# Mixture of experts on one core: the next expert's rows turned and split behind the fifth chunk of this expert's first products

## The chip, the cores and the metric

The kernel runs on one core of one Trainium2 chip. The metric is the time of one launch on the device, in microseconds (us). The engines of the core run side by side, each through its own list of instructions, and wait for one another by semaphores: TensorE (PE) for matrix products, VectorE (DVE) and ScalarE (ACT) for element-wise work, GpSimd (POOL), and SyncE (SP), which here only issues transfers (DMA).

## The reference

The program is two transformer blocks on 512 tokens of width 1024. The first has two layers of mixed attention and a gated MLP. The second has a recurrent part, banded and memory attention, and ends in a routed mixture of 32 experts. Only the experts matter here. Each token goes to two experts; expert e computes, for the rows `xb` routed to it,

```
g = xb @ w_gate[e]                      # 1024 -> 512
u = xb @ w_up[e]                        # 1024 -> 512
y = (silu(g) * u) @ w_down[e]           # 512 -> 1024
```

`y` is weighted by the router and added to the token's row; a last norm follows. All is in float32.

## The kernel before

A product of float32 numbers is made of three products of rounded parts: each operand is split into a high part, its value rounded, and a low part, the rest; high by high, high by low and low by high are summed. So each weight and each row goes through a copy on ACT (high part) and a subtraction on DVE (low part) first.

The experts are run one after another with up to 96 rows each (`CAP`). The weights of one expert come in 12 chunks of 512 KB: eight of gate and up together (`e_gu`, 128 of the 1024 input features each) and four of down (`e_dn`). SP loads each into one of 28 raw buffers (`ewr`), ACT casts the high part `ewh` (L1478), DVE subtracts the low part `ewl` (L1480). Of `ewh` and of `ewl` there are three buffers each (`NH`), so a chunk's cast can only start when the products of the chunk three places before it are done.

One expert's run (`Experts.run`) has these steps:

- Turning: the gathered rows `gx` (96 x 1024) are transposed on PE, eight pieces into two PSUM banks `s` (L1500), and split into `xh` on ACT (L186) and `xl` on DVE (L187). Then the gather for the expert two places on is issued on POOL (`then()`).
- First products: for each of the eight chunks six matmuls, into `pg` (gate, L1512) and `pu` (up, L1513).
- `z`: ACT takes the silu of `pg` (L1515), DVE multiplies it by `pu` (L1516).
- Second products: `z` is transposed on PE into `pt` (L1520, four pieces) and split into `zh` on ACT and `zl` on DVE (L186, L187). Then 24 matmuls with the four down chunks (L1530).
- ACT scales the result into `y` (L1539, two halves), POOL adds it to the output in memory (L1540).

`run` is a generator. Its `yield`s cut it into pieces, and the loop in `moe_block` calls the pieces of two experts in turn, so that the first two chunks of expert e+1 stand ahead of the down products of expert e. The five PSUM banks for products are given out in turn, so `pu` of expert e+1 gets the bank of `pg` of expert e, and must wait until the silu has read it.

The order of the calls is not yet the order on the engines. The framework schedules the recorded instructions by its own estimate of when each can run, fixes one list for each engine, and adds the waits. The lists shown below are those.

Of the kernel before, what the change touches and what calls it, by code (L numbers as in the profile page):

```python
# [1281 lines left out]
NE = 32  # L1282
CAP = 96
LAST = 2
# [161 lines left out]
class Experts:  # L1446
# [41 lines left out]
    def run(self, i, gu, dn, sidx, w, r, y=None, then=lambda: None):  # L1488


        B, nc, wk = self.B, self.B.nc, self.wk
        mm = nc.tensor.matmul
        flat = lambda t: t.rearrange("p k n -> p (k n)")
        xh = wk.tile([P, KD, CAP], F32R, tag="xh", name="xh", bufs=self.nw)
        xl = wk.tile([P, KD, CAP], F32R, tag="xl", name="xl", bufs=self.nw)
        for a in range(2):
            pt = B.bank("t", "s")[:, :4 * CAP]
            for j in range(4):
                k = 4 * a + j
                nc.tensor.transpose(pt[:, j * CAP:(j + 1) * CAP], self.gx[i][:, k * P:(k + 1) * P],  # L1500
                                    B.ident[:CAP, :CAP])
            s = slice(4 * a, 4 * a + 4)
            B.split(pt, flat(xh[:, s]), flat(xl[:, s]))
        then()
        pg, pu = B.acc()[:CAP], B.acc()[:CAP]
        for k in range(KD):
            if k == 2:
                yield
            wh, wlo = gu(k)
            for x, ww, last in ((xh, wh, False), (xh, wlo, False), (xl, wh, k == KD - 1)):  # L1510
                first = k == 0 and ww is wh and x is xh
                mm(pg, x[:, k], ww[:, :T], start=first, stop=last)  # L1512
                mm(pu, x[:, k], ww[:, T:], start=first, stop=last)  # L1513
        z = wk.tile([CAP, T], F32, tag="z", name="z", bufs=self.nw)
        self.silu = nc.scalar.activation(z, pg, AF.Silu, scale=r)  # L1515
        nc.vector.scalar_tensor_tensor(z, pu, r, z, op0=ALU.mult, op1=ALU.mult)  # L1516
        yield
        pt = B.pst()[:, :4 * CAP]
        for j in range(4):
            nc.tensor.transpose(pt[:, j * CAP:(j + 1) * CAP], z[:, j * P:(j + 1) * P], B.ident[:CAP, :CAP])  # L1520
        zh = wk.tile([P, 4, CAP], F32R, tag="zh", name="zh", bufs=self.nw)
        zl = wk.tile([P, 4, CAP], F32R, tag="zl", name="zl", bufs=self.nw)
        self.zl = B.split(pt, flat(zh), flat(zl))
        pd = [B.acc()[:CAP], B.acc()[:CAP]]
        for k in range(4):
            wh, wlo = dn(k)
            for x, ww, last in ((zh, wh, False), (zh, wlo, False), (zl, wh, k == 3)):
                first = k == 0 and ww is wh and x is zh
                for a in range(2):
                    mm(pd[a], x[:, k], ww[:, a * T:(a + 1) * T], start=first, stop=last)  # L1530
        if y is not None:
            y.append([wk.tile([CAP, D], F32R, tag="y" + g, name="y" + g, bufs=LAST) for g in "hl"])
            for a in range(2):
                B.gsplit(pd[a], w, [t[:, a * T:(a + 1) * T] for t in y[-1]])
            yield
            return
        y = wk.tile([CAP, D], F32, tag="y", name="y", bufs=self.nw)
        for a in range(2):
            nc.scalar.mul(y[:, a * T:(a + 1) * T], pd[a], w)  # L1539
        nc.gpsimd.indirect_dma_start(out=self.y2[:, :], out_offset=bass.IndirectOffsetOnAxis(ap=sidx, axis=0),  # L1540
                                     in_=y, in_offset=None, bounds_check=T - 1, oob_is_err=False,
                                     compute_op=ALU.add)
        yield
# [73 lines left out]
def moe_block(B, dense, out):  # L1617

    tc, nc, I = B.tc, B.nc, B.I
    with ExitStack() as cx:  # L1620
# [66 lines left out]
        def run(e, y=None):  # L1687
            then = (lambda: ex.gather(e % NG, idx[:, e + NG:e + NG + 1])) if e + NG < NE else lambda: None
            return ex.run(e % NG, lambda k: ex.load(gu[e * D + k * P:e * D + (k + 1) * P, :]),
                   lambda k: ex.load(dn[e * T + k * P:e * T + (k + 1) * P, :]), idx[:, e:e + 1], wl[:, 0, e:e + 1],  # L1690
                          wl[:, 1, e:e + 1], y, then)
# [9 lines left out]

        pick, ys = [], []
        prev, now = None, run(0)
        next(now)
        for e in range(NE):
            next(now)
            ex.hold = None, None
            if e + 1 < NE:
                then = run(e + 1, ys if e + 1 >= NE - LAST else None)
                next(then)  # L1710
            if e < NE - 2:
                next(now)
            elif e == NE - 1:
                next(prev)
                next(now)
            prev, now = now, then
# [30 lines left out]
def build(tc, I, out):  # L1747
    with ExitStack() as ctx:
        dr = ctx.enter_context(tc.tile_pool(name="drm", bufs=1, space=bass.MemoryType.DRAM))
        B = Block(tc, I, ctx)  # L1750
        B.kd = dr.tile([KD, P, 256], F32, name="kd")
        B.vd = dr.tile([2, P, D], F32, name="vd")
        first = first_block(B)
        moe_block(B, lambda h3: second_block_dense(B, first, h3), out)
# [158 lines left out]
```

## Time and profile before

| what | value |
|---|---|
| three timed runs | 2436.26, 2440.36, 2441.43 us; median 2440.36 us |
| profiled execution, its own time | 2438.89 us |
| its span, first to last instruction | 2437.1 us |
| PE busy over the span | 2284.5 us (94%) |
| DVE busy | 1768.8 us (73%) |
| ACT busy | 1402.7 us (58%) |
| chain that ended last | PE 71%, DVE 11%, issue 8%, ACT 6%, DMA 3% |

The launch's own time is 1.8 us longer than the span. The chain of work that ended last is followed back from the last instruction, at each step to what released it. The experts take the last quarter of the span, from about 1824 to about 2420 us. In the rows below a time is counted from the start of the span; "idle before" is how long the engine had nothing running just before the row, and the arrow names what ended that.

### The profile page before, as it was taken

The numbers are of one execution on the slowest core, as the hardware profiler recorded it, in microseconds if no ns is written. First come the engines' busy times: TensorE is split into PE (matmuls) and PEld (weight loads), VectorE is DVE, ScalarE is ACT, GpSimd is POOL, SyncE is SP. The second block draws the span as 40 slices with busy tenths as digits, with TensorE's granted clock in tenths as the row PEclk, the third lists the DMA queues.
The fourth block names the chain that finished last, engine by engine and source line by source line (L and its number), as shares of the span: only waits on it lengthen the run. The fifth ranks groups of instructions, "written<-read, shape, count | busy, mean of one in ns | idle before, by whom it ended". The sixth has DMA issues, their size and how long they took to land.

```text
span 2437.1 us, 33968 instructions
## 1 busy us (share of the span) xinstructions
PE 2284.5 (94%) x12341; PEld 1877.2 (77%) x12341; DVE 1768.8 (73%) x3246; ACT 1402.7 (58%) x2279; POOL 142.9 (6%) x136
## 2 busy tenths in 40 slices
PE   6888989999999899899999998999979999999998
PEld 6878968888888789788888887978756666666665
DVE  7899878745756897664434467687658888888888
ACT  4576764322333867643223446655427888888886
POOL 0000000000000000000000000100011111111110
PEclk9999999999999999999999999999979999999999
DMA  9623415635643111032233232214379999999992
GB/s 325 190 87 105 140 60 170 202 115 180 195 143 93 44 62 55 33 104 95 80 111 95 80 98 79 61 57 151 110 270 325 362 364 358 357 354 353 353 348 93
DMA packets 131872, 417.83 MB, mean 171 GB/s; under 512 B 22937, under 2 KB 30105, under 8 KB 131696
## 3 DMA queue, kind: packets, MB, share of 16 engines
q1 hardware_dynamic: 122832, 401.03, 48.2%
q0 software_dynamic: 8864, 14.54, 2.2%
q8 instruction: 99, 1.62, 0.3%
q14 instruction: 77, 0.63, 0.1%
HBM read 411.46 MB, written 20.19 MB: 177 GB/s over the span
## 4 chain that ended last, share of the span: by engine, by line
PE 71%; DVE 11%; issue 8%; ACT 6%; DMA 3%; SPq 0%; POOL 0%; DVEq 0%; ACTq 0%; POOLq 0%
PE acc L191 12%; PE acc L192 12%; PE acc L193 12%; PE acc L1512 8%; PE acc L1530 7%; PE acc L1513 7%; PE acc L490 2%; PE acc L491 2%; PE acc L492 2%; DVE wl L177 2%; PE s L396 1%; PE pv L457 1%; PE pt L444 1%; DVE wm L384 1%; ACT wh L176 1%
## 5 line engine op out<-in xcount | busy, mean ns | idle before, releaser
L176 ACT CAST wh<-wr 128x1024 fp32r<-128x1024 f32 (+2 forms) x284 | 272.9, 963 | 454.1 <-PE acc L192 356.0
L1480 DVE TENSOR_TENSOR ewl<-ewr,ewh 128x1024 fp32r<-128x1024 f32 x384 | 463.7, 1221 | 72.7 <-ACT ewh L1478 51.2
L177 DVE TENSOR_TENSOR wl<-wr,wh 128x1024 fp32r<-128x1024 f32 (+2 forms) x284 | 317.2, 1118 | 229.2 <-ACT wh L176 222.7
L1478 ACT CAST ewh<-ewr 128x1024 fp32r<-128x1024 f32 x384 | 397.6, 1052 | 88.5 <-PE acc L1513 54.3
L191 PE MATMUL acc<-hh,wh 128*128 128x512 f32 (+1 forms) x1088 | 411.0, 380 | 5.2 <-ACT hh L186 4.1
L192 PE MATMUL acc<-hl,wh 128*128 128x512 f32 (+1 forms) x1088 | 414.4, 381 | 0.0
L193 PE MATMUL acc<-hh,wl 128*128 128x512 f32 (+1 forms) x1088 | 411.5, 379 | 1.9 <-DVE wl L177 1.9
L191 PEld LDWEIGHTS acc<-hh,wh 128*128 128x128 f32 x1088 | 204.6, 189 | 48.3 <-ACT hh L186 4.7
L193 PEld LDWEIGHTS acc<-hh,wl 128*128 128x128 f32 x1088 | 206.1, 189 | 42.6 <-DVE wl L177 2.7
L192 PEld LDWEIGHTS acc<-hl,wh 128*128 128x128 f32 x1088 | 205.8, 189 | 40.2 <-DVE hl L187 0.2
L490 PE MATMUL acc<-wh,hh 128*128 128x256 f32 (+1 forms) x768 | 228.9, 298 | 0.0
L491 PE MATMUL acc<-wl,hh 128*128 128x256 f32 (+1 forms) x768 | 221.4, 288 | 0.0
L492 PE MATMUL acc<-wh,hl 128*128 128x256 f32 (+1 forms) x768 | 221.0, 288 | 0.0
L491 PEld LDWEIGHTS acc<-wl,hh 128*128 128x128 f32 x768 | 151.0, 197 | 2.8
L490 PEld LDWEIGHTS acc<-wh,hh 128*128 128x128 f32 x768 | 151.5, 197 | 2.0
L492 PEld LDWEIGHTS acc<-wh,hl 128*128 128x128 f32 x768 | 150.6, 196 | 0.0
L401 ACT ACTIVATE e<-e,st 128x128 f32<-128x128 f32 (+2 forms) x192 | 107.6, 561 | 69.7 <-DVE st L399 67.8
L384 DVE SCALAR_TENSOR_TENSOR wm<-wm,scb 128x1024 f32<-128x1024 f32 x96 | 116.8, 1221 | 37.3 <-DMA wm<-in_w_mod_dram 36.7
L192 PE MATMUL acc<-zl,wh 128*128 128x512 f32 (+1 forms) x363 | 141.3, 389 | 0.0
L191 PE MATMUL acc<-zh,wh 128*128 128x512 f32 (+1 forms) x363 | 141.0, 389 | 0.0
L193 PE MATMUL acc<-zh,wl 128*128 128x512 f32 (+1 forms) x363 | 140.2, 386 | 0.0
L1512 PE MATMUL acc<-ewh,xh 128*96 128x512 f32 x256 | 103.9, 406 | 12.6 <-ACT xh L186 12.6
(418 smaller groups left out, 4575.6 us busy)
## 6 DMA issues: line engine op xcount, KB each, us to landing
ewr<-in_e_gu_dram SPq DMA_DIRECT2D x256, 512.0 KB, 7.2
ewr<-in_e_dn_dram SPq DMA_DIRECT2D x128, 512.0 KB, 8.5
wm<-in_w_mod_dram SPq DMA_DIRECT2D x96, 512.0 KB, 4.2
wr<-in_w_up_dram SPq DMA_DIRECT2D x88, 512.0 KB, 3.5
wr<-in_w_qkv_dram SPq DMA_DIRECT2D x56, 512.0 KB, 3.5
wr<-in_w_down_dram SPq DMA_DIRECT2D x32, 512.0 KB, 3.6
wr<-in_w_out_dram SPq DMA_DIRECT2D x16, 512.0 KB, 3.5
wr<-in_w_down_dram SPq DMA_DIRECT2D x32, 192.0 KB, 2.3
```

The lines of the kernel that those rows point to most:

```text
L176: nc.scalar.copy(hi, raw)
L177: nc.vector.tensor_sub(lo, raw, hi)
L191: mm(ps, wh, ah, start=first, stop=False)
L192: mm(ps, wh, al, start=False, stop=False)
L193: mm(ps, wl, ah, start=False, stop=last)
L490: mm(ps, ah[:, s], wh[:, w], start=k == 0, stop=False)
L491: mm(ps, ah[:, s], wl[:, w], start=False, stop=False)
L492: mm(ps, al[:, s], wh[:, w], start=False, stop=k == KD - 1)
L1478: nc.scalar.copy(hi, raw)
L1480: nc.vector.tensor_sub(lo, raw, hi)
L1512: mm(pg, x[:, k], ww[:, :T], start=first, stop=last)
L1513: mm(pu, x[:, k], ww[:, T:], start=first, stop=last)
```

## The change

The `yield`s are set anew and the loop is changed with them. The turning of expert e+1 becomes a piece of its own, called after the fifth chunk of expert e's first products; its first two chunks are still called after the eighth. For expert 0 the turning and the first two chunks are called one after the other.

```diff
         then()
+        yield
         pg, pu = B.acc()[:CAP], B.acc()[:CAP]
         for k in range(KD):
-            if k == 2:
+            if k in (2, 5):
                 yield
...
         prev, now = None, run(0)
         next(now)
+        next(now)
         for e in range(NE):
+            next(now)
+            if e + 1 < NE:
+                then = run(e + 1, ys if e + 1 >= NE - LAST else None)
+                next(then)
             next(now)
             ex.hold = None, None
             if e + 1 < NE:
-                then = run(e + 1, ys if e + 1 >= NE - LAST else None)
                 next(then)
             if e < NE - 2:
                 next(now)
```

Below is what the engines' lists make of it, for an expert in the middle. Lines of the changed kernel are one higher there: L1513 and L1514 are the products of L1512 and L1513, L1521 is L1520, L1531 is L1530.

PE before, from the last matmuls of one expert's eighth chunk: `s` is the next expert's turning, then come its first chunk and, inside that, the transposes `pt` of this expert's z.

```order
L1513 MATMUL acc<-ewh,xl 96x512
L1500 MATMUL s<-c_ident,gx_17363 128x96 x6
L1512 MATMUL acc<-ewh,xh 96x512
L1513 MATMUL acc<-ewh,xh 96x512
L1512 MATMUL acc<-ewl,xh 96x512
L1513 MATMUL acc<-ewl,xh 96x512
L1520 MATMUL pt<-c_ident,z 128x96 x4
L1512 MATMUL acc<-ewh,xl 96x512
L1513 MATMUL acc<-ewh,xl 96x512
```

Eight more matmuls, and the down products, follow there: two of the eight transposes of `s` stand earlier, in the fifth chunk. PE in the changed kernel, from the second half of the next expert's first chunk (its three matmuls into `pg` stand ahead of the three into `pu`) to the first down products (L1531):

```order
L1514 MATMUL acc<-ewh,xh 96x512
L1514 MATMUL acc<-ewl,xh 96x512
L1514 MATMUL acc<-ewh,xl 96x512
L1513 MATMUL acc<-ewh,xh 96x512
L1514 MATMUL acc<-ewh,xh 96x512
L1513 MATMUL acc<-ewl,xh 96x512
L1514 MATMUL acc<-ewl,xh 96x512
L1513 MATMUL acc<-ewh,xl 96x512
L1514 MATMUL acc<-ewh,xl 96x512
L1521 MATMUL pt<-c_ident,z 128x96 x4
L1500 MATMUL s<-c_ident,gx_17363 128x96 x8
L1531 MATMUL acc<-ewh,zh 96x512 x2
```

The turning no longer stands ahead of its own expert's products: the list has it between the transposes of z and the down products, and it is that of the expert two places on. The transposes of z went from the middle of the next expert's first chunk to behind its second.

ACT before, from one silu (L1515) to the next: twelve casts of weight chunks (L1478), with the splits `xh` and `zh` (L186) and `y` between them.

```order
L1515 ACTIVATE z<-acc,lw 96x512
L186 CAST xh<-s 128x384 x2
L1478 CAST ewh<-ewr 128x1024
L186 CAST zh<-pt 128x384
L1478 CAST ewh<-ewr 128x1024 x5
L1539 ACTIVATE y<-acc,lw 96x512 x2
L1478 CAST ewh<-ewr 128x1024 x6
```

ACT in the changed kernel, from silu (L1516) to the next; the three casts behind it are those of the first three down chunks.

```order
L1516 ACTIVATE z<-acc,lw 96x512
L1478 CAST ewh<-ewr 128x1024 x3
L186 CAST zh<-pt 128x384
L186 CAST xh<-s 128x384 x2
L1478 CAST ewh<-ewr 128x1024 x3
L1540 ACTIVATE y<-acc,lw 96x512 x2
L1478 CAST ewh<-ewr 128x1024 x6
```

The split `zh` stood behind one cast of a down chunk and stands behind three now; DVE's list has the same shape, with `zl` behind one subtraction of a down chunk before and behind three now.

## Rows read from the trace of the kernel before

**Rows 1.** Busy time by stretch of 20 us, with granted clock, DMA share, GB/s

```profile
core 0: us, PE busy (x) PEld busy (x) DVE busy (x) ACT busy (x) POOL busy (x), PEclk, DMA share, GB/s
1820.00:1840.00 20.00, 16.92 (x63) 11.47 (x64) 12.88 (x19) 10.18 (x13) 2.60 (x2) 0.69 0.87 303
...
1960.00:1980.00 20.00, 19.59 (x92) 13.76 (x91) 17.78 (x18) 16.82 (x21) 2.49 (x2) 1.00 1.02 373
...
2380.00:2400.00 20.00, 19.59 (x92) 13.74 (x91) 17.81 (x18) 16.57 (x20) 1.43 (x1) 1.00 0.35 114
```

**Rows 2.** Tile ewr, 2370 to 2390 us: the last weight loads and their landing

```profile
L1485 SPq DMA_DIRECT2D ewr<-in_e_dn_dram x4: 328/328/328, 2369.9 to 2373.4; - x4
...
DMA to landing us min/median/max: 5.6/5.7/5.9
```

**Rows 3.** ACT in order of time: the last two casts of weights

```profile
2413.96 2.00 ACT L1478 CAST ewh<-ewr 128x1024 fp32r<-128x1024 f32 x2
```

**Rows 4.** Waits of PE, 1860 to 2395 us: total, times, longest

```profile
PE acc L1512 <- ACT xh L186: 12.3, 30, 0.4
```

**Rows 5.** PE in order of time, one expert: start, length, instruction, idle before

```profile
2061.41 0.40 PE L1513 MATMUL acc<-ewh,xl 128*96 128x512 f32 x1
2061.64 0.66 PE L1500 MATMUL s<-c_ident,gx 96*128 96x96 f32 x6
2062.71 0.47 PE L1512 MATMUL acc<-ewh,xh 128*96 128x512 f32 x1 [0.41 <-ACT xh L186]
...
2063.71 0.49 PE L1520 MATMUL pt<-c_ident,z 96*128 96x96 f32 x4
2063.99 0.46 PE L1512 MATMUL acc<-ewh,xl 128*96 128x512 f32 x1
...
2065.67 0.40 PE L1513 MATMUL acc<-ewh,xl 128*96 128x512 f32 x1
2065.90 0.62 PE L1530 MATMUL acc<-ewh,zh 128*96 128x512 f32 x2
...
2070.98 0.62 PE L1530 MATMUL acc<-ewh,zl 128*96 128x512 f32 x2
...
2074.92 0.47 PE L1512 MATMUL acc<-ewl,xh 128*96 128x512 f32 x1
...
2079.85 0.39 PE L1513 MATMUL acc<-ewh,xl 128*96 128x512 f32 x1
```

**Rows 6.** ACT in order of time, the same expert

```profile
2061.61 0.69 ACT L1515 ACTIVATE z<-acc,lw 96x512 f32<-96x512 f32 x1
2062.19 0.84 ACT L186 CAST xh<-s 128x384 fp32r<-128x384 f32 x2
...
2064.24 0.48 ACT L186 CAST zh<-pt 128x384 fp32r<-128x384 f32 x1 [0.25 <-PE pt L1520]
...
2066.10 1.05 ACT L1478 CAST ewh<-ewr 128x1024 fp32r<-128x1024 f32 x1 [0.34 <-PE acc L1513]
...
2071.41 1.26 ACT L1539 ACTIVATE y<-acc,lw 96x512 f32<-96x512 f32 x2
2072.57 2.94 ACT L1478 CAST ewh<-ewr 128x1024 fp32r<-128x1024 f32 x3
```

**Rows 7.** DVE in order of time, the same expert

```profile
2062.68 0.74 DVE L1516 SCALAR_TENSOR_TENSOR z<-acc,lw,z 96x512 f32<-96x512 f32 x1
...
2064.27 1.21 DVE L1480 TENSOR_TENSOR ewl<-ewr,ewh 128x1024 fp32r<-128x1024 f32 x1
2065.40 0.55 DVE L187 TENSOR_TENSOR zl<-pt,zh 128x384 fp32r<-128x384 f32 x1
...
2073.64 4.79 DVE L1480 TENSOR_TENSOR ewl<-ewr,ewh 128x1024 fp32r<-128x1024 f32 x4 [1.08 <-DMA ewr<-in_e_gu_dram]
```

**Rows 8.** PE in order of time: the transposes of z of expert 0

```profile
1841.26 0.38 PE L1520 MATMUL pt<-c_ident,z 96*128 96x96 f32 x2 [1.01 <-DVE z L1516]
```

**Rows 9.** PE in order of time: a matmul while the granted clock was down

```profile
1828.01 0.63 PE L1513 MATMUL acc<-ewh,xh 128*96 128x512 f32 x1
```

## The prediction

> **What bounds the kernel now.** I read the busy time by stretch first, then the last loads, the waits of PE, and one expert on PE, ACT and DVE in order of time.
>
> From 1840 to 2400 us every stretch of 20 us has PE busy for over 18 us at a granted clock of 1.00, as in [rows 1]; but the loads are just as busy, with a DMA share of 1.02 at 373 GB/s. Either could set the end. The last loads decide it: the last weights are issued at 2373.4 us and land some 5.7 us later [rows 2], at 2379, and their casts run from 2414 us on [rows 3]. The data is 35 us early, so the engines set the pace. PE has one wait that repeats: 30 times 0.41 us, 12.3 us in all, the first chunk of an expert waiting for its turned rows `xh` [rows 4].
>
> One expert on PE [rows 5], with three marks. G is the start of its last first-product matmul, 2061.41. M is the start of the last matmul of the next expert's second chunk, 2065.67. D is the start of the last down product, 2070.98 + 0.23 = 2071.21 (the row holds two). The next G is 2079.85. So G to M is 4.26 us, M to D 5.54, D to the next G 8.64; together 18.44 us. The 24 down products from 2065.90 to 2071.21 stand 5.31 / 23 = 0.231 us apart; four transposes, 2063.71 to 2063.99, 0.07 apart. In G to M PE does six transposes, then stands still until 2062.71. The row shows 0.41 idle, since the transposes' ends are modelled; their issue takes 6 x 0.07 = 0.42, so about 0.65 us is lost. A restarted matmul takes 0.08 longer (0.47 against 0.39).
>
> **The change, part by part.** The work is the same, instruction for instruction; only the lists differ. I go through the three legs.
>
> *G to M.* The turning and the transposes of z leave this leg: twelve matmuls remain. The first three go into `pg`, whose bank is free. The fourth, into `pu`, needs the bank that silu reads: silu runs from G + 0.20 to G + 0.89 [rows 6], and PE follows an ACT result by about 0.05 (xh's first half, started 2062.19 and about 0.47 long, released PE at 2062.71). That gives G + 0.94, against G + 0.92 from the matmuls before: no stall to speak of. Eight more matmuls give M at G + 0.94 + 8 x 0.231 = G + 2.79. Saved: 4.26 - 2.79 = 1.47 us. It is more than the 0.65 us of waiting, because the transposes have moved into the next leg.
>
> *M to D.* Behind M stand twelve transposes: PE is through at M + 0.23 + 12 x 0.07 = M + 1.07. Their inputs are early: z is done on DVE at 2062.68 + 0.74 [rows 7], G + 2.01, before M; the gather was issued two experts, 37 us, ahead as before, and a weight chunk, larger than it, lands in 5.7 us. The down products then need `zh`. On ACT's list `zh` stands behind the casts of the first three down chunks. The third of these reuses the buffer of the next expert's second chunk, so it cannot start before that chunk's last matmul, M, has ended. The trace has this very cast, at 2066.10 = M + 0.43, released by PE [rows 6]; there `zh`, at 2064.24, was already through, since it stood behind one cast only. Now it comes after it. Three casts in a row take 2.94 with the last 1.05 long, so one follows the other by 0.945: `zh` starts at M + 1.38, ends 0.48 later, and the down products start at M + 1.91. Stall: 0.84.
>
> Then the low half. The subtraction for the third chunk starts 0.05 after its cast ends, M + 1.53; `zl` starts 1.13 behind it (2064.27 to 2065.40 [rows 7]), M + 2.66, takes 0.55, and reaches PE at M + 3.26. PE has four products without it, 0.31 + 3 x 0.23 = 1.00, and is there at M + 2.91. Stall: 0.35. Twenty products follow: D at M + 3.26 + 0.08 + 19 x 0.231 = M + 7.73. Lost: 7.73 - 5.54 = 2.19 us.
>
> *D to the next G.* Two transposes of the turning leave the fifth chunk, but that buys nothing. The cast of the fifth chunk stands behind `y`: `y` at D + 0.20, the casts at D + 1.36 [rows 6], the subtraction at D + 2.43, about 1.2 long [rows 7]; PE's first product with that low part is at D + 3.71 [rows 5]. Without the transposes PE would come at D + 0.23 + 14 x 0.231 = D + 3.46 and wait. Change: 0.
>
> *The sum.* -1.47 + 2.19 = +0.72 us per expert, 19.16 instead of 18.44. It holds where an expert's down products stand between the products of the next and there is a turning to place: 29 boundaries, the 30 waits of [rows 4] less the last, into expert 31, behind which no down products come. 29 x 0.72 = 20.9 us. The ends I put at 0 with 2 us to either side: the first boundary was already slow (PE waits 1.01 us for z there [rows 8]); the last saves about 1.47; and at the very end z of expert 31 is transposed ahead of expert 30's down products, which costs about its silu and its product, 0.69 + 0.74. The profiled execution took 2438.89 us, which gives 2459.8. The median of the three runs, 2440.36, is 1.5 above that; I forecast 2460.
>
> *Queues it moves past.* SP's loads come in the same order of chunks; POOL still alternates gathers and adds. ACT and DVE have the same number of instructions. Behind the cast that waits on ACT are queued `zh`, both `xh` and the fourth down chunk's cast: the first is what PE waits for, `xh` is for two experts on, and the fourth chunk is needed 18 products after the first.
>
> *The bounds.* No row shows the new neighbours side by side. From below: if `zl` came in time, say because the third subtraction were taken behind it, D would be at M + 1.91 + 0.08 + 23 x 0.231 = M + 7.30, +0.29 per expert, 2439 + 8 = 2447. From above: if nothing overlapped and cast, subtraction and silu took their full lengths (1.05 for 0.945, 1.21 for 1.13, and the silu 0.1 late behind a cast that ends just ahead of it), +1.0 per expert, 2439 + 29 = 2468. I take 0.72, the value nearest to the rows of the same instructions.
>
> **The rivals.**
>
> *Faster: the split of z is ready when PE wants it.* Mechanism: PE loses the 0.65 us of waiting for `xh`, and ACT gets to `zh` before the third down chunk's cast. Then the down products start behind the twelve transposes, M to D is 0.23 + 0.84 + 0.06 + 5.31 = 6.44, and an expert gains 1.47 - 0.90 = 0.57 us: 2439 - 17 = 2422. For it: `xh` is the only wait of PE that repeats, and it does go. Against: the list has three casts ahead, and in [rows 6] each entry starts after the one ahead of it. It decides where the new waits with their restarts, 0.84 + 0.08 + 0.35 + 0.08 = 1.35 in my sum, come to less than 0.63 us.
>
> *No change: the loads are the limit.* At a DMA share of 1.02, a faster or slower order on PE would change only how long it waits, 2439. Against: the 35 us by which the last data is early, and not one wait of PE for data in [rows 4].
>
> *Much slower: the clock drops.* PE would stand still twice per expert instead of once. A matmul at the lower of its two levels (1.2 and 2.4 GHz) is 0.63 long [rows 9] against 0.39. If the 24 down products behind the waits ran so, it would cost 24 x 0.24 = 5.8 us per expert, 168 us in all: 2607. Against: the clock in [rows 1] stays at 1.00 through 30 waits of this size, one per expert. The Trainium skill, "TensorE: Matmul & The Clock Gate", section "A second HAM failure mode: psum-queue depth-cycling", reports a kernel in which frequent short idling between groups of matmuls let the clock swing between its two levels. By that page the time would be near this rival's; the trace does not agree for one such gap per expert, and no run here shows two.
>
> **How the numbers follow.** Forecast 0.84, faster 0.07, no change 0.06, clock 0.03. What this kernel's measurement can tell from no change is about 0.2%, 5 us. All of the forecast's own range, 2447 to 2468 with some 2 us for the ends, is slower by more than that, and so is the clock's: slower 0.87, same 0.06, faster 0.07. The range is 2444 to 2472, which takes in the two bounds and the uncertain ends; it leaves out the two other sides.
>
> **What the profile would show.** Right: 29 experts at a period of 19.1 to 19.2; no wait of the first gate products for `xh`, in its place a wait of the first down product for `zh` of about 0.8 and one of the fifth or sixth down product for `zl` of about 0.35; the third down cast at M + 0.43 with `zh` directly behind it; clock 1.00; the last weights still landing far ahead of their casts. The forecast is wrong if `zh` starts before that cast, if PE's fourth matmul behind G waits visibly for silu, or if PE waits for weights.

## The result and the profile after

| | median us | runs | profiled execution's span |
|---|---|---|---|
| before | 2440.72 | 2436.26 to 2441.43 (4) | 2437.1 |
| after | 2462.63 | 2458.88 to 2464.67 (4) | 2461.5 |

The ratio is 1.009, 95% interval 1.0073 to 1.0108: slower by 22 us, where the forecast was 2460 in a range of 2444 to 2472, slower.

The list of PE's waits, 1860 to 2420 us (total, times, longest), answers to [rows 4]:

```profile
PE acc L1531 <- ACT zh L186: 15.1, 29, 0.5
PE acc L1531 <- DVE zl L187: 5.4, 29, 0.2
```

The wait for `xh` is gone. Two others stand in its place, 29 times each, at the down products (L1531). Their sum, 20.5, is 8.2 us more than the 12.3 that went, and the kernel lost 22: the list alone doesn't give the size. For that, one expert is read on PE in order of time (start, length, instruction, idle before), as in [rows 5]:

```profile
2067.30 0.47 PE L1513 MATMUL acc<-ewl,xh 128*96 128x512 f32 x1
...
2072.20 0.39 PE L1514 MATMUL acc<-ewh,xl 128*96 128x512 f32 x1
...
2073.14 0.48 PE L1514 MATMUL acc<-ewh,xh 128*96 128x512 f32 x1
...
2075.04 0.39 PE L1514 MATMUL acc<-ewh,xl 128*96 128x512 f32 x1
2075.27 0.49 PE L1521 MATMUL pt<-c_ident,z 96*128 96x96 f32 x4
2075.60 0.82 PE L1500 MATMUL s<-c_ident,gx 96*128 96x96 f32 x8
2076.94 0.70 PE L1531 MATMUL acc<-ewh,zh 128*96 128x512 f32 x2 [0.52 <-ACT zh L186]
2077.48 0.63 PE L1531 MATMUL acc<-ewl,zh 128*96 128x512 f32 x2
2078.30 0.71 PE L1531 MATMUL acc<-ewh,zl 128*96 128x512 f32 x2 [0.19 <-DVE zl L187]
```

G is 2072.20 and M is 2075.04: 2.84 us, where it was 4.26. Behind M come the twelve transposes, then nothing until 2076.94, four products, and again nothing until 2078.30. The ACT list of the same stretch answers to [rows 6]:

```profile
2063.78 1.26 ACT L1540 ACTIVATE y<-acc,lw 96x512 f32<-96x512 f32 x2
...
2072.40 0.68 ACT L1516 ACTIVATE z<-acc,lw 96x512 f32<-96x512 f32 x1
2072.98 2.17 ACT L1478 CAST ewh<-ewr 128x1024 fp32r<-128x1024 f32 x2
2075.47 1.05 ACT L1478 CAST ewh<-ewr 128x1024 fp32r<-128x1024 f32 x1 [0.31 <-PE acc L1514]
2076.42 0.47 ACT L186 CAST zh<-pt 128x384 fp32r<-128x384 f32 x1
...
2082.99 1.26 ACT L1540 ACTIVATE y<-acc,lw 96x512 f32<-96x512 f32 x2
```

The third down chunk's cast starts at M + 0.43, released by PE, and `zh` directly behind it, M + 1.38. On DVE, answering to [rows 7]:

```profile
2073.47 0.74 DVE L1517 SCALAR_TENSOR_TENSOR z<-acc,lw,z 96x512 f32<-96x512 f32 x1
2074.13 3.64 DVE L1480 TENSOR_TENSOR ewl<-ewr,ewh 128x1024 fp32r<-128x1024 f32 x3
2077.69 0.55 DVE L187 TENSOR_TENSOR zl<-pt,zh 128x384 fp32r<-128x384 f32 x1
```

Three subtractions end to end, then `zl`. The chain of work that ended last (start, length, what) tells which of the two waits set the pace:

```profile
2075.20 0.24 PE acc L1514
2075.47 1.06 ACT ewh L1478
2076.55 1.23 DVE ewl L1480
2077.77 0.48 DVE zl L187
2078.30 4.67 PE acc L1531 x19
2082.99 0.25 ACT y L1540
```

It goes from M over the third cast, the third subtraction and `zl` to the down products. `zh`, which has the longer wait in the list above, isn't in it. Loads and clock, answering to [rows 1]:

```profile
1960.00:1980.00 20.00, 19.21 (x96) 13.20 (x95) 17.19 (x17) 15.94 (x19) 3.37 (x2) 1.00 0.97 340
...
2400.00:2420.00 20.00, 19.22 (x88) 12.96 (x88) 17.16 (x18) 15.98 (x19) 1.42 (x1) 1.00 0.32 106
```

The clock is 1.00. The loads run slower than before: 340 against 373 GB/s in this stretch, and 343 against 356 over 1860 to 2320 us, which takes in whole experts. In both kernels SP waits there for nothing but the subtraction on DVE that frees a raw buffer, and it comes later now. The last weights are issued and cast as follows (SP's queue, then ACT), answering to [rows 2, 3]:

```profile
2385.28 12.55 SPq L1485 DMA_DIRECT2D ewr<-in_e_dn_dram  x8
```

```profile
2438.78 1.99 ACT L1478 CAST ewh<-ewr 128x1024 fp32r<-128x1024 f32 x2
```

The last is issued at 2397.5 and lands 5.7 later; the casts of the last two begin some 36 us after that, where it was 35 before.

The size of the loss is read from the 32 rows of silu, of which the view of one line gives the first and the last start. Before:

```profile
L1515 ACT ACTIVATE z<-acc,lw x32: 683/685/687, 1839.4 to 2406.1; 96x512 f32<-96x512 f32 x32
```

After:

```profile
L1516 ACT ACTIVATE z<-acc,lw x32: 683/684/686, 1841.8 to 2429.5; 96x512 f32<-96x512 f32 x32
```

From first to last that is 566.7 us before and 587.7 after, 21.0 more. Below I call this the stage, and the usual distance of two silu rows the period (18.43 before, 19.22 after). The stage is the better measure of an edit to the experts: the first silu started between 1835.8 and 1850.7 us in the profiled runs of this study, and nearly all that lies ahead of it is in lines that no edit touched.

### The profile page after: what moved, and what is told of

Read it like the earlier page. It is cut to its first block, busy times and chain, and to the rows that moved or that the text cites. A ratio compares the mean times of both kernels' runs of the same rounds, so it can differ in the third digit from the quotient of the medians.

```text
span 2461.5 us, 33968 instructions
## 1 busy us (share of the span) xinstructions
PE 2299.3 (93%) x12341; PEld 1872.2 (76%) x12341; DVE 1769.5 (72%) x3246; ACT 1400.2 (57%) x2279; POOL 167.3 (7%) x136
## 5 line engine op out<-in xcount | busy, mean ns | idle before, releaser
L1478 ACT CAST ewh<-ewr 128x1024 fp32r<-128x1024 f32 x384 | 396.8, 1050 | 122.8 <-PE acc L1531 59.8
L554 POOL TENSOR_SCALAR op<-ones 64x512 fp32r<-64x512 f32 x20 | 32.1, 1603 | 1266.7 <-PE s L396 692.8
```

Of the source, the lines that this page charges most:

```text
L1478: nc.scalar.copy(hi, raw)
```

## The experiments

My theory was the prediction's: the split of z stands behind three down chunks on ACT and DVE and comes too late. Rivals: the reuse of a buffer alone (the third cast's wait for M), the new calls or the twelve transposes in one place, the loads, the clock.

| run | median us | ratio to before, 95% | stage us | period us |
|---|---|---|---|---|
| both splits forward | 2436.56 | 0.9977 to 1.0007 | 563.4 | 18.21 |
| zh alone forward | 2494.05 | 1.0196 to 1.0266 | 609.3 | 19.94 |
| zl alone forward | 2448.68 | 1.0023 to 1.0059 | 574.4 | 18.78 |
| four buffers | 2450.86 | 1.0032 to 1.0063 | 578.4 | 18.91 |
| y later | 2459.82 | 1.0060 to 1.0100 | 578.6 | 18.92 |
| z transposed early | 2435.98 | 0.9969 to 0.9995 | 559.8 | 18.08 |
| both splits forward, y later | 2441.60 | 0.9988 to 1.0015 | 563.1 | 17.95, then 19.5 |
| z early, y later | 2435.42 | 0.9967 to 0.9989 | 559.5 | 17.77, then 19.5 |
| before, z split late | 2471.85 | 1.0102 to 1.0149 | 591.0 | 19.25 |
| z early, y later, even lists | 2424.26 | 0.9920 to 0.9956 | 546.5 | 17.76, then 18.0 |

### Both splits of z forward

```diff
-        self.zl = B.split(pt, flat(zh), flat(zl))
+        zs = nc.scalar.copy(flat(zh), pt)
+        self.zl = nc.vector.tensor_sub(flat(zl), pt, flat(zh))
+        free = self.hold
...
+            self.hold = (zs, self.zl) if k >= 2 else free
             wh, wlo = dn(k)
+            self.hold = free
```

`hold` queues a chunk's cast and subtraction behind the named instructions.

> The changed kernel with one thing set: on ACT the third down chunk's cast stands behind zh, on DVE its subtraction behind zl; each split of z now has two down chunks ahead instead of three. Theory (the split of z is queued too far back): zh starts 0.53 us behind the transposes of z, M + 0.76, PE starts the down products at M + 1.28, zl follows at M + 1.5 and is not waited for, M to D 6.74, period 2.84 + 6.74 + 8.61 = 18.19 us, 2441 - 29 x 0.25 = 2433 us (2428 to 2440), faster than the kernel before; the wait for zl is gone, that for zh is under 0.3. Rival (the twelve transposes in one place, or the clock behind two gaps, make the loss): M to D stays near 7.7 and the time near 2463. Rival (loads limit): PE waits for data and the time is not under 2441.

Measured: 2436.56 us. In its chain of work one expert reads:

```profile
2057.34 0.33 PE pt L1521 x4
2057.68 0.58 PE s L1500 x7
2058.25 5.78 PE acc L1535 x24
```

and on ACT and on DVE:

```profile
2057.71 0.48 ACT L1524 CAST zh<-pt 128x384 fp32r<-128x384 f32 x1 [0.64 <-PE pt L1521]
```

```profile
2056.05 2.35 DVE L1480 TENSOR_TENSOR ewl<-ewr,ewh 128x1024 fp32r<-128x1024 f32 x2
2058.32 0.55 DVE L1525 TENSOR_TENSOR zl<-pt,zh 128x384 fp32r<-128x384 f32 x1
```

M is 2057.18 - 0.23 = 2056.95. `zh` starts at M + 0.76 and the down products at M + 1.29, as worked out; in this expert the chain stays on PE from silu to silu. Eleven of the twelve transposes are where the changed kernel has them. (The last of the turning comes later: in this expert at 2067.11, in the fifth chunk of the next one's products; in the next expert four products behind the others.) So their place is not the loss. The run takes 26 us off the changed kernel, and with that the time can't be told from the kernel before, where I had expected 8 us less. 24 periods lie near 18.2; three of the six behind them are 19.9, 5 us in all. That came up again below.

### Each split forward alone

```diff
...
+            self.hold = (zs if k == 2 else free[0], free[1])
+            wd.append(dn(k))
...
+        with B.tc.issue_after(self.sub.ins):
+            self.zl = nc.vector.tensor_sub(flat(zl), pt, flat(zh))
...
```

Here `zh` is ahead of the third cast and `zl` behind the third subtraction.

> The changed kernel with zh ahead of the third down chunk's cast, but zl left behind its subtraction. Rival (the wait for zh, 15.1 us in the list of waits against 5.4 for zl, is the larger part, so removing it gives back about 15 us): 2448. Theory (the down products end by what comes last, the low half): the third cast, taken behind zh, ends at M + 2.24, its subtraction ends 1.2 later, zl starts at M + 3.45 and reaches PE at M + 4.06; M to D 8.53, period 19.98, 2463 + 29 x 0.77 = 2485 us (2475 to 2492), slower than the changed kernel although its wait for zh shrinks.

```diff
...
+            self.hold = (None, self.zl) if k >= 2 else free
             wh, wlo = dn(k)
...
```

Here only `zl` is ahead.

> The changed kernel with zl ahead of the third down chunk's subtraction, zh left behind its cast. Theory: zh still at M + 1.38, the down products start at M + 1.91; zl at M + 1.90 comes in time; M to D 7.29, period 18.74, 2463 - 29 x 0.47 = 2449 us (2444 to 2455): the wait for zh stays at about 0.5, that for zl is gone. Rival (zl's wait is small, 0.19 per expert, so this gives back 5.4 us only): 2457. Rival (position of zl plays no part): 2463.

Measured: 2494.05 and 2448.68. In the first, on ACT, DVE and PE in turn:

```profile
2062.24 0.48 ACT L1524 CAST zh<-pt 128x384 fp32r<-128x384 f32 x1 [0.66 <-PE pt L1521]
2062.61 1.05 ACT L1478 CAST ewh<-ewr 128x1024 fp32r<-128x1024 f32 x1
```

```profile
2063.70 1.23 DVE L1480 TENSOR_TENSOR ewl<-ewr,ewh 128x1024 fp32r<-128x1024 f32 x1 [0.80 <-ACT ewh L1478]
2064.84 0.55 DVE L1531 TENSOR_TENSOR zl<-pt,zh 128x384 fp32r<-128x384 f32 x1
```

```profile
2065.44 0.70 PE L1538 MATMUL acc<-ewh,zl 128*96 128x512 f32 x2 [1.43 <-DVE zl L1531]
```

The wait for `zh` is gone and that for `zl` has grown from 0.19 to 1.43: the third cast, pushed back, pushes back the subtraction that `zl` stands behind. Taking away the largest wait of the list in this way made the kernel 31 us slower, 22 of them in the stage. The period is 19.94, against 19.98 expected; the time is 2 us above the expected range all the same. The 9 us between 2485 and 2494 are outside the periods, 6.5 of them behind the last silu (38.5 us to the end of the span against 32.0). There PE stands still for 1.34 us (`z`), works for 1.9 and stands still for 1.41 (`zl`), and then the granted clock is down:

```profile
2454.00:2459.00 5.00, 5.00 (x12) 3.35 (x13) 1.43 (x2) 2.09 (x2) 0.00 (x0) 0.50 0.00 0
```

This is the lower of the two levels; up to 2451 and again from 2459 the clock is 1.00. Twelve products take 5.2 us there instead of 2.8. In the second run PE's one repeated wait, 1860 to 2390 us, is

```profile
PE acc L1535 <- ACT zh L1524: 15.1, 29, 0.5
```

the same 15.1 as in the changed kernel, yet 14 us are gained, from taking away the smaller entry. The list makes it small: in the changed kernel the four products ahead of `zl` would have been followed by the next at 2077.48 + 0.46 = 2077.94, and that started at 2078.30, so 0.36 us were lost and 0.08 more by the restart, where the list has 0.19. Both signs and both periods are the theory's. With `zl` out of the way `zh` does set the pace: the run with both forward has a period 0.57 shorter still.

### Four buffers

```diff
-NR1 = 13
-NH = 3
+NR1 = 11
+NH = 4
```

> The changed kernel with four buffers for the high and four for the low halves instead of three each (two raw buffers fewer, 26 for 28); the lists are the same. The third down cast needs no longer wait for the next expert's second chunk. Rival (that wait, the reuse of a buffer, is the cause): zh comes 0.36 us earlier and so do the products, 2463 - 29 x 0.36 = 2453 us or less. Theory (three chunks ahead of the split, DVE's subtractions end to end, are the cause): zh starts at M + 1.0 and the down products at M + 1.55, but zl still starts at M + 2.65, behind three subtractions of 1.21 us that follow z without a gap; PE waits for it longer, M to D stays 7.75, 2463 us (2458 to 2467).

Measured: 2450.86, the rival's number, but not for its reason. I was wrong that the lists stay the same: the framework let ACT run one chunk further ahead, so behind silu now stand the second, third and fourth down chunks, and the last of these, four places behind the next expert's second chunk, waits for M just as before. On ACT, with M at 2052.95:

```profile
2053.38 1.05 ACT L1478 CAST ewh<-ewr 128x1024 fp32r<-128x1024 f32 x1 [0.31 <-PE acc L1514]
2054.33 0.47 ACT L186 CAST zh<-pt 128x384 fp32r<-128x384 f32 x1
```

PE's waits are the same to the digit (15.1 and 5.4, 29 each). What was gained, 0.31 per period, is the third leg: the fifth chunk's low half is no longer late. So the run doesn't tell the reuse of the buffer from the three chunks in a row. The rows of the changed kernel do in part: its third subtraction starts at 2076.55, directly behind the cast, while two subtractions from 2074.13 on at 1.12 to 1.13 us each would have left DVE free at about 2076.4. Worked out so, the tie to M costs some 0.16 us per expert, and the three in a row the rest; no run here shows that by itself.

### y later: the third leg alone

```diff
...
+        yield
         y = wk.tile([CAP, D], F32, tag="y", name="y", bufs=self.nw)
...
             next(now)
+            if 0 < e < NE - 1:
+                next(prev)
...
```

> The changed kernel with the calls for y made behind the next expert's fifth chunk: on ACT the fifth chunk's cast then stands between the two halves of y, no longer behind both; nothing else moves. It tests the third leg alone, D to the next G, which was costed at 8.64 with PE waiting about 0.25 for the fifth chunk's low half and 0.08 for the restart. Theory: the cast starts some 0.6 us earlier, the wait goes, the leg is 8.31, period 18.91, 2463 - 29 x 0.30 = 2454 us (2449 to 2459); zh and zl are waited for as before (15.1 and 5.4). Rival (that wait is hidden behind the later ones, so it is only moved): 2463. Rival (y later holds back the output's adds or a PSUM bank, so PE waits there): over 2463.

Measured: 2459.82. The stage is 578.6, 9.1 us shorter, and the period 18.92 against 18.91 expected: a wait that shows in no list (the restarted matmul at 2067.30 is its only trace) cost 0.30 each time. The time fell by 3 us only and is 1 us above the expected range: in the profiled run the first silu came 6.4 us later (1848.2 against 1841.8), ahead of the first place where the edit acts. Why it came later no run here shows.

### z transposed early

```diff
-            if k in (2, 5):
+            if k in (1, 2, 5):
...
         self.zl = B.split(pt, flat(zh), flat(zl))
+        yield
...
```

The loop calls the transposes of z between the next expert's first and second chunk.

> The changed kernel with the calls cut finer: z is transposed between the next expert's first and second chunk, as in the kernel before, while the turning stays away from G. The lists put the transposes of z in the middle of the second chunk, zh and zl behind two down chunks, and the turning behind the fourth down product. Theory: PE does not wait for xh; zh starts behind two casts at G + 2.96, the down products at G + 3.5, zl is there before the turning is through; D at G + 9.45, period 18.06, 2441 - 29 x 0.38 = 2430 us, and some 5 more if the last eight experts are uneven as in the run with both splits forward: 2434 (2426 to 2440). Rival (the turning costs its 0.56 us wherever it stands and the split of z decides nothing more): 2437, as with both splits forward. Rival (loads limit): 2441.

Measured: 2435.98, period 18.08 against 18.06, the stage 6.9 us shorter than before; three late periods near 19.9 again. With y later as well, and with both splits forward and y later:

> Both splits of z forward (as in the first of these runs, 2437) and y's calls behind the fifth chunk. Theory (the legs add up): period 18.2 - 0.30 = 17.9, 2437 - 9 = 2428 us (2422 to 2434), faster than the kernel before by 0.5%. Rival (the loads, which ran at a DMA share near 1, become the limit below 18.2 us per expert): not under 2435, with PE waiting for casts that wait for data.

> z transposed between the next expert's first and second chunk, and y's calls behind the fifth chunk. Theory (each leg's gain is its own): period 18.06 - 0.30 = 17.76, 2441 - 29 x 0.68 = 2421 us, up to 2426 if the last eight experts are uneven; faster than the kernel before by 0.6 to 0.8%. Rival (loads limit): as the run with both splits forward, 2435.

Measured: 2441.60 and 2435.42, both misses: 8 and 9 us above the expected ends, 2434 and 2426, and at the rival's number. Over the first 21 experts the legs add up, 17.95 and 17.77 us against 17.9 and 17.76. Then eight periods of 19.5 take it back. There the lists had slipped: the next expert's second chunk is cast behind silu instead of ahead of it. In the second of these runs, 1845 to 2430 us, PE's waits that come more than twice are

```profile
PE acc L1513 <- DVE ewl L1480: 4.4, 8, 0.6
PE acc L1514 <- ACT z L1516: 2.8, 9, 0.3
```

Neither names a load, but the rival (loads that run dry) would also show late, so it had a run of its own below. The profiled execution of this second run, with its first silu at 1850.7, was the slowest of twelve (2430.2 to 2444.0).

### The kernel before, with z split late

```diff
...
-        self.zl = B.split(pt, flat(zh), flat(zl))
+        wd = [dn(k) for k in range(3 if self.nh > 1 else 1)]
+        with B.tc.issue_after(self.cast.ins):
+            nc.scalar.copy(flat(zh), pt)
+        with B.tc.issue_after(self.sub.ins):
+            self.zl = nc.vector.tensor_sub(flat(zl), pt, flat(zh))
...
```

> The kernel before, its calls and their order untouched, with one thing set: zh behind the third down chunk's cast on ACT, zl behind its subtraction on DVE. The framework then makes the same lists of it, for the experts in the middle, as of the changed kernel (the turning goes behind the transposes of z by itself). Theory (the late split of z is the whole loss, whatever brings it about): period 19.2, 2463 us (2457 to 2468). Rival (the new calls themselves, their place in the loop, cost the time): 2441.

Measured: 2471.85. PE waits as in the changed kernel:

```profile
2062.27 0.70 PE L1534 MATMUL acc<-ewh,zh 128*96 128x512 f32 x2 [0.52 <-ACT zh L1525]
2063.62 0.71 PE L1534 MATMUL acc<-ewh,zl 128*96 128x512 f32 x2 [0.19 <-DVE zl L1527]
```

The period is 19.25, that of the changed kernel, with the loop and its pieces those of before: the new calls as such are not the loss. The turning has moved behind the transposes of z here too, so this run alone doesn't tell its place from the late split; the run with both splits forward does. The time is 4 us above the expected range. The 9 us by which it exceeds that of the changed kernel are at the edges: the first period 21.7 against 19.2, the end behind the last silu 36.5 against 32.0, and a first silu 1.7 later.

### Even lists

```diff
...
+        ahead = [gu(k) for k in range(2)] if self.nh > 1 else []
+        yield
...
-        self.silu = nc.scalar.activation(z, pg, AF.Silu, scale=r)
+        with nullcontext() if self.cast is None else B.tc.issue_after(self.cast.ins):
+            self.silu = nc.scalar.activation(z, pg, AF.Silu, scale=r)
...
```

Added to the version with z early and y later.

> As the run with z transposed early and y later (2435; 17.77 us per expert over the first 21, 19.5 over the last eight, whose lists have slipped by one chunk), with the next expert's first two chunks cast ahead of silu in every expert, so that the slip can't happen. The last eight still have the turning in one place and y ahead of the fifth chunk's cast, as in the run with both splits forward, 18.2 to 18.3. Theory (what was lost there was the list and not the loads): 2435 - 8 x 1.2 = 2425 us (2419 to 2431), 0.6% faster than the kernel before. Rival (at under 18 us per expert the loads run dry towards the end, and the 19.5 was that): 2435, with the last eight experts at 19.5 again.

Measured: 2424.26 (2421.01 to 2427.91), 0.6% faster than the kernel before and 38 us faster than the changed one. The late periods are 18.0. The 19.5 was the list. From 1840 on, in stretches of 160, 200 and 180 us:

```profile
1840.00:2000.00 160.00, 160.00 (x759) 111.42 (x758) 146.75 (x145) 138.48 (x163) 30.71 (x18) 1.00 1.00 362
2000.00:2200.00 200.00, 200.00 (x948) 138.98 (x947) 183.90 (x182) 173.18 (x204) 37.42 (x22) 1.00 0.98 355
2200.00:2380.00 180.00, 179.28 (x843) 124.64 (x842) 163.49 (x162) 153.29 (x180) 23.52 (x18) 1.00 0.97 352
```

PE is busy all the time and waits for no load. But the loads no longer keep pace; they live on their lead. SP's waits from 1860 to 2320 us are, before and here,

```profile
SPq L1485 <- DVE ewl L1480: 338.5, 300, 2.3
```

```profile
SPq L1485 <- DMA ewr<-in_e_gu_dram: 187.6, 170, 3.2
SPq L1485 <- DMA ewr<-in_e_dn_dram: 102.8, 86, 3.0
SPq L1485 <- DVE ewl L1480: 60.1, 89, 1.6
```

Before, SP waited for buffers alone, and each chunk was issued 41.5 us ahead of its cast throughout. Here it waits mostly for transfers, the rate stays at 356 GB/s, that of before, though PE is 4% faster, and the lead falls: 38.7 us for the chunk cast at 1966.7, 22.5 for the one cast at 2323.5, twenty experts later. Chunks of gate and up took 12.7 us to land (median; 7.3 before). The loads had become the slower side, at 18.65 us per expert against 17.84; by these numbers, an estimate, some twelve more experts would have used up the lead.

## Why the prediction was right

- **G to M.** Forecast 2.79, measured 2.84. The fourth matmul restarts at G + 0.94, as worked out, but that restart is 0.48 long, and 0.05 of the 0.08 which the prediction charged elsewhere and left out here ("no stall to speak of") show in the leg: of the terms that set the sum, the one that was mis-sized most.
- **M to D.** Forecast 7.73; D is 2082.99 - 0.20 = 2082.79, M + 7.75. The third cast at M + 0.43, `zh` at M + 1.38, `zl` on PE at M + 3.26 are as forecast, the down products at M + 1.90 (forecast 1.91). The transposes were mis-sized without effect: they are 0.08 apart and not 0.07 (eight take 0.82, the last of them 0.25), so PE is through them at M + 1.21 and not M + 1.07, and loses 0.69 rather than 0.84 to `zh`, which sets the start either way. The list has 0.52 and 0.19 for the two waits where 0.8 and 0.35 were forecast, since it counts idle time from modelled ends.
- **D to the next G.** Forecast unchanged at 8.64; from the D of the expert before, 2063.78 - 0.20 = 2063.58, to 2072.20 it is 8.62. Taking two transposes away bought nothing, since the fifth chunk's low half was waited for; the run with y later shows the hidden 0.30.
- **The sum.** 29 x 0.72 = 20.9 was forecast. The stage grew by 21.0: 29 periods longer by 0.785 or 22.8, less 0.35 in the first (19.52 to 19.17) and 1.46 in the last (12.60 to 11.14; forecast 1.47). That the stage agrees with the sum to 0.1 is luck: the periods cost 1.9 us more than forecast, and the first and the last one, which the sum leaves out, cost 1.8 less. Behind the last silu 1.0 is added (31.0 to 32.0; forecast 1.4), which makes 22.0 against the 20.9 forecast with the ends at 0. The spans differ by 24.4; the other 2.4 are a later first silu, 1.8 of them there already at the first turning (1823.97 against 1822.18), ahead of what was changed.
- **The bounds.** The lower one, `zl` in time and `zh` late, was priced at 2447; the run with `zl` alone forward is that case, 2449.
- **The rivals.** Faster: its condition, waits under 0.63 us, wasn't met in the changed kernel; with both splits forward its mechanism appears, but M to D is 6.69 and not 6.44, since `zh` follows the transposes of z by 0.53. No change: PE never waited for a load, not even at 17.77 us per expert, but from about 18.2 on the loads fell behind it and only their lead kept that from showing; the prediction's reason, that the data was early, was right for this kernel and not a sign that the loads could go faster. The clock: 1.00 in every stretch from 1840 to 2440, now with two gaps per expert. The run with `zh` alone forward has a gap of 1.43 in each expert, and its stretch from 1860 to 2420 us reads

```profile
1860.00:2420.00 560.00, 517.82 (x2360) 350.21 (x2360) 460.86 (x451) 432.15 (x507) 80.38 (x55) 1.00 0.93 330
```

The Trainium skill's "TensorE: Matmul & The Clock Gate", section "A second HAM failure mode: psum-queue depth-cycling", which stood behind that rival, tells of a clock that swings where PE idles shortly and often between groups of matmuls. These runs don't agree for gaps of 0.2 to 1.4 us, one or two in some 19 us. Two gaps close together are another matter: the stretch at a granted clock of 0.50 behind the last silu of the same run came after 1.34 and 1.41 us of standing still, 1.9 us apart.

What was argued and not shown: why the framework's lists slip in the last eight experts (what they cost was measured), and how the loss divides between the wait for M and the three chunks in a row.

## What to carry to other kernels

Moving work away from one wait moves it in front of another, so ask what then stands ahead of the next result on each in-order queue. A list of waits is no list of gains: follow the chain, since the longer wait here was off it, and the edit that took it away alone cost 31 us, while the shorter was on it. A compute engine that never waits for data doesn't show that the loads keep up: ask what the load queue itself waits for, buffers or transfers, and whether its lead holds. And when a scheduler makes the lists, count an instruction's place in every repetition, not in a middle one only.

## What was not expected

- A matmul behind a gap takes 0.47 to 0.48 us against 0.39, also where no idle time is shown: that was the only sign of a wait of 0.30 per expert.
- The DMA share doesn't tell whether the loads have room: it was 0.99 from 1860 to 2320 us in the kernel before, whose lead held, and in the run with even lists, whose lead shrank. The rate followed the pace of PE only up to 356 GB/s: 331 at 19.94 us per expert, 343 at 19.22, 356 at 18.43, and 356 still at 17.77.
